# Where the stores of the first expert table are issued, and when the gathered block's pairs and rows are worked on, in a hybrid decoder step

## The chip, the core and the metric

The kernel runs on one core of a Trainium2 chip. The core has five engines with queues of their own: TensorE (PE, matrix products; its weight loads are listed as PEld), VectorE (DVE), ScalarE (ACT), GpSimd (POOL) and SyncE (SP, which only issues transfers). Each engine runs its instructions in the order of its own queue, and waits on semaphores for the others. Matrix products land in PSUM, a small memory of eight banks; all other tiles lie in SBUF; tables and intermediate results of some size lie in DRAM and are moved by DMA. A DMA is issued by an engine's queue (SP, ACT or POOL) and carried by 16 DMA engines.

The metric is the time of one execution on the device in microseconds (us); of several runs the median.

## What is computed

One inference step of a one-layer decoder for 512 prompt rows and 8 sample rows of 1024 columns. The change lies in the PEER part, a layer of 16384 small experts of which every row uses 128 (8 heads, 16 experts each):

```python
q = (xb @ peer_wq).reshape(PEER_BLOCK, PEER_HEADS, 2, PEER_QDIM // 2)
s1 = jnp.einsum('thd,hnd->thn', q[:, :, 0], peer_k1)
s2 = jnp.einsum('thd,hnd->thn', q[:, :, 1], peer_k2)
v1, i1 = lax.top_k(s1, PEER_TOPK)
v2, i2 = lax.top_k(s2, PEER_TOPK)
cand = (v1[..., :, None] + v2[..., None, :]).reshape(PEER_BLOCK, PEER_HEADS, -1)
cidx = (i1[..., :, None] * N_KEYS + i2[..., None, :]).reshape(PEER_BLOCK, PEER_HEADS, -1)
top, pos = lax.top_k(cand, PEER_TOPK)
idx = jnp.take_along_axis(cidx, pos, axis=-1)
gate = jax.nn.softmax(top.astype(jnp.float32), axis=-1).astype(xb.dtype)
act = jax.nn.gelu(jnp.einsum('thkd,td->thk', peer_u[idx], xb), approximate=False)
return jnp.einsum('thk,thkd->td', gate * act, peer_v[idx])
```

Before it in the layer come two recurrent branches (Mamba-2 and RWKV-7) and their projections, after it a small gated projection and a norm.

## The kernel before, in words

The rows are five row blocks: 0 to 3 are the 512 prompt rows, 128 each, and 4 the 8 sample rows. PEER is computed in two ways. Row blocks 0, 1, 2 and 4 (392 rows, `ND`) go the dense way: every expert's activation is computed for every row, and a gate that is zero for experts not chosen is multiplied in. Row block 3 goes the gathered way: its 128 chosen experts per row are fetched from DRAM row by row.

*The first table's loop* (L1531) runs over the 128 table blocks `i1` of `peer_u`, 128 experts each. `u_in(i1 + 1)` (L1488) loads the next block's tile `ur` (512 KB, two buffers), PE transposes it in two halves of four products into PSUM (tiles `tr` and `psB`), ACT casts each half to the high part `uh`, and DVE subtracts to get the low part `ul`. "Split" below is this pair of DVE instructions. `u_out` (L1503) makes 24 products per block (three for each of eight column groups) into `psA`; ACT applies the GELU into `ge` (three buffers), and SP stores `ge` to `ge_d` in DRAM (L1516). From block 80 (`NU`) on, the gates exist: then DVE multiplies them in ahead of the store, and the last 16 blocks stay in SBUF.

*The gates.* `pairs(pool, c, gate)` (L1321) finds, for a row block, the 16 best of 50 candidate pairs per head and their expert numbers (`ij`) and softmax weights; it is a generator in seven pieces, almost all DVE work: top-16 searches (`best16`, L1272), small index arithmetic, and two times three operations over 128x2048 elements (L1362 to L1365). `scatter` (L1376) runs `pairs` of a dense row block and then places the gates into a dense array: for four rows at a time DVE makes one-hot tiles (L1412, L1416), PE multiplies them (L1395), ACT copies the result into a staging tile `stg` (L1397), and after every 32 rows SP stores `stg`, 2 MB, to `G_d` in DRAM (L1402; 13 stores in all, the last of 0.5 MB). The pieces of the four scatters are spread over table blocks 0 to 75 by the counter `nsc` up to `NSC` (L1527, L1542): 133 pieces in 76 blocks.

*The gathered row block.* Its `pairs` run in one go ahead of the loop (`run`, L1432, called at L1440); from them come the expert numbers `e3`. `gathered` (L1447) fetches a row of 128 experts (tile `gr`, 512 KB, an indirect DMA of POOL, L1453), and DVE multiplies and sums it with the row block (L1462), for 128 rows of `peer_u` and then 128 of `peer_v`. `gather_to` (L1475) says how far it is: 80 rows over blocks 0 to 79, 70 more over blocks 80 to 127, the rest in the second table's loop (L1573), which works through `peer_v` in the same way.

*What sets the order.* A framework schedules each engine's instructions by their place in the program and their dependences, so a call's place sets the order only roughly. Each engine then keeps that order: an SP load stands behind every store that SP has ahead of it, and a store of `ge` can't go before its GELU.

The lines quoted here are the parts that the steps below use; line numbers are those of the profile.

Of the kernel before, what the change touches and what calls it, by code (L numbers as in the profile page):

```python
# [8 lines left out]
F32 = mybir.dt.float32  # L9
# [5 lines left out]
OP = mybir.AluOpType  # L15
# [15 lines left out]
def tile_hybrid(ctx: ExitStack, tc, x_prompt, x_sample, p_prompt, p_sample, state_ssm, state_conv,  # L31
# [13 lines left out]
    def f(ap):  # L45
        return ap.bitcast(F32)
# [1234 lines left out]
    with tc.tile_pool(name="qp", bufs=2, reuse_waits="tile") as qp:  # L1281
        for h in range(8):
# [9 lines left out]
            for s_ in range(2):  # L1292
                c0 = (h * 2 + s_) * P
                raw = dw.tile([P, D], F32, name="ur")
# [81 lines left out]
    def scatter(pool, c):  # L1376
# [13 lines left out]
        def place(t, one, stg):  # L1390
# [9 lines left out]
            if q + 4 == m:  # L1400
                a = off[c] + t - q
                nc.sync.dma_start(G_d[:, :, a:a + m, :].rearrange("c p t l -> p c (t l)"),  # L1402
                                  stg[:, :, :m, :].rearrange("p c t l -> p c (t l)"))
# [28 lines left out]
    def run(gen):  # L1432

        while True:
            try:
                next(gen)
            except StopIteration as e:
                return e.value

    ij = run(pairs(sc, 3, g3))  # L1440
    V.scalar_tensor_tensor(ij[:, 0], ij[:, 0], float(P), ij[:, 1], op0=OP.mult, op1=OP.add)
    S.copy(e3, ij[:, 0])
# [32 lines left out]
    def gather_to(n):  # L1475
        while rows_done[0] < n:
            next(gg, None)
            rows_done[0] += 1


    uT, vT = peer_u[0], peer_v[0]
    NU = 80
    GU1, GU2 = 80, 70
    NK = 16
    ge_d = dram.tile([P - NK, P, ND], F32, name="ge_d")
    ges = {}

    def u_in(i1):  # L1488

        raw = dw.tile([P, D], F32, name="ur")  # L1490
        nc.sync.dma_start(raw, uT[i1 * P:(i1 + 1) * P])
        uh = du.tile([P, KD, P], F32R, name="uh")
        ul = du.tile([P, KD, P], F32R, name="ul")
        for q in range(2):
            qs_ = slice(q * 4, q * 4 + 4)
            ps = pa.tile([P, 4, P], F32, name="psB") if q else pt.tile([P, 4, P], F32, name="tr")
            for k in range(4):
                T.transpose(ps[:, k], raw[:, (q * 4 + k) * P:(q * 4 + k + 1) * P], identf)
            S.copy(uh[:, qs_], ps)  # L1499
            V.tensor_tensor(ul[:, qs_], ps, f(uh[:, qs_]), op=OP.subtract)  # L1500
        return uh, ul

    def u_out(i1, u, gt):  # L1503
# [9 lines left out]
        if keep:  # L1513
            ges[i1] = a
        else:
            nc.sync.dma_start(ge_d[i1], a)  # L1516
# [6 lines left out]
    def scatters():  # L1523
        for c in (0, 1, 2, 4):
            yield from scatter(sc, c)
    sg_ = scatters()
    NSC = 4 * 6 + W0 + 3 * WAIT + 3 * 32 + 2  # L1527
    nsc = 0
    u = u_in(0)
    vbx = ExitStack()  # L1530
    for i1 in range(P):  # L1531
# [9 lines left out]
        if i1 < NU:  # L1541
# [3 lines left out]
            gather_to((i1 + 1) * GU1 // NU)  # L1545
# [171 lines left out]
```

## Time and profile before

| | us |
|---|---|
| median of 3 runs | 2987.49 |
| lowest, highest | 2976.54, 2988.84 |
| profiled execution, its own time | 2980.14 |
| its span, first to last instruction | 2978.4 |
| first table's loop, blocks 0 to 127 | about 1500 to 2322 |
| of that, blocks 0 to 79 | about 1500 to 2081 |
| second table's loop | 2322 to 2882 |

The profile is of one execution. Its views: a page with the busy share of each engine; a table of stretches, in us from the span's start; lists of who waited for whom; a timeline of each engine; and groups of instructions by line. "x24" is a count of instructions. A wait "<-DVE ul L1500" names what ended it. Durations of neighbours on an engine may overlap, since an instruction begins before the last one has drained.

### The profile page before, as it was taken

What the parts mean: (1) busy time and instruction counts of PE and PEld (TensorE: products, weight loads), DVE (VectorE), ACT (ScalarE), POOL (GpSimd) and SP (SyncE); (2) the same over time, 40 slices, a digit from 0 to 9 for tenths busy, and PEclk for the clock granted to TensorE, in tenths of its full rate; (3) what the DMA queues carried; (4) which work ended last, traced back from release to release, by engine and by line L of the source; (5) the groups of instructions that cost most, each with busy time, mean ns of one, the idle gap of its engine ahead of it and who ended that gap; (6) DMA issues with size and microseconds to landing.
All of it is one profiled execution on the core that took longest, in us unless ns stands there. A gap on an engine that the chain in (4) does not pass through costs nothing. (4 is left out here: it accounts for less than half of the span.)

```text
span 2978.4 us, 52286 instructions
## 1 busy us (share of the span) xinstructions
PE 2785.6 (94%) x20189; PEld 2594.3 (87%) x20192; DVE 2243.9 (75%) x5555; ACT 1001.0 (34%) x2027; POOL 350.2 (12%) x310
## 2 busy tenths in 40 slices
PE   5999999898997999999969999999999999999998
PEld 4988888787886888977959999999999999999986
DVE  5868787877877775345999999884777787787746
ACT  2443333334332333232223433332322333333332
POOL 0000000000000012100001111111222334322100
PEclk9999989898897999999979999999999999999999
DMA  3314252433415366541326877677998989899830
GB/s 93 80 46 109 79 122 51 107 83 87 116 44 119 81 182 186 160 135 65 89 96 218 253 232 227 217 264 224 338 333 302 332 311 328 322 317 326 276 113 29
DMA packets 446995, 528.15 MB, mean 177 GB/s; under 512 B 95464, under 2 KB 357243, under 8 KB 446705
## 3 DMA queue, kind: packets, MB, share of 16 engines
q1 hardware_dynamic: 386153, 377.42, 41.1%
q0 software_dynamic: 38304, 139.22, 13.8%
q10 hardware_dynamic: 22288, 8.16, 1.1%
q8 instruction: 159, 2.61, 0.4%
q14 instruction: 91, 0.75, 0.1%
HBM read 447.83 MB, written 77.14 MB: 176 GB/s over the span
## 5 line engine op out<-in xcount | busy, mean ns | idle before, releaser
L95 PE MATMUL ps<-hhi,whi 128*128 128x260 f32 (+1 forms) x1456 | 440.6, 303 | 7.5 <-ACT ctail L410 2.8
L97 PE MATMUL ps<-hhi,wlo 128*128 128x260 f32 (+1 forms) x1456 | 441.1, 303 | 0.8 <-DVE wlo L79 0.8
L96 PE MATMUL ps<-hlo,whi 128*128 128x260 f32 (+1 forms) x1456 | 441.2, 303 | 0.0
L97 PE MATMUL psA<-h2h,ul 128*128 128x392 f32 x1024 | 351.8, 344 | 21.6 <-DVE ul L1500 21.6
L95 PE MATMUL psA<-h2h,uh 128*128 128x392 f32 x1024 | 363.7, 355 | 0.4 <-ACT uh L1499 0.2
L97 PE MATMUL av<-ah,vl 128*128 128x392 f32 x1024 | 351.7, 344 | 1.8 <-DVE vl L79 1.8
L96 PE MATMUL psA<-h2l,uh 128*128 128x392 f32 x1024 | 352.9, 345 | 0.0
L95 PE MATMUL av<-ah,vh 128*128 128x392 f32 x1024 | 349.4, 341 | 3.2 <-ACT vh L78 3.2
L96 PE MATMUL av<-al,vh 128*128 128x392 f32 x1024 | 350.0, 342 | 1.8 <-DVE al L79 1.8
L95 PEld LDWEIGHTS ps<-hhi,whi 128*128 128x128 f32 (+1 forms) x1456 | 284.3, 195 | 20.6 <-issue 6.0
L97 PEld LDWEIGHTS ps<-hhi,wlo 128*128 128x128 f32 (+1 forms) x1456 | 283.7, 195 | 11.8 <-issue 4.5
L96 PEld LDWEIGHTS ps<-hlo,whi 128*128 128x128 f32 (+1 forms) x1456 | 284.1, 195 | 11.3 <-issue 5.5
L78 ACT CAST vh<-vr 128x1024 fp32r<-128x1024 f32 x128 | 134.1, 1050 | 316.1 <-PE av L96 150.8
L1453 POOL DMA_INDIRECT gr<-in_peer_v_dram,e x128 | 177.5, 1387 | 375.3 <-DVE o L1468 357.7
L1453 POOL DMA_INDIRECT gr<-in_peer_u_dram,e x128 | 125.9, 984 | 794.2 <-DVE junk L1462 501.4
L97 PEld LDWEIGHTS psA<-h2h,ul 128*128 128x128 f32 x1024 | 195.5, 191 | 22.1 <-DVE ul L1500 22.1
L78 ACT CAST whi<-wraw 128x1024 fp32r<-128x1024 f32 (+1 forms) x115 | 120.0, 1043 | 279.0 <-PE ps L96 231.4
L95 PEld LDWEIGHTS psA<-h2h,uh 128*128 128x128 f32 x1024 | 195.2, 191 | 1.6 <-ACT uh L1499 1.6
L95 PEld LDWEIGHTS av<-ah,vh 128*128 128x128 f32 x1024 | 193.0, 189 | 3.9 <-ACT vh L78 3.5
L79 DVE TENSOR_TENSOR vl<-vr,vh 128x1024 fp32r<-128x1024 f32 x128 | 156.2, 1222 | 52.7 <-ACT vh L78 52.6
L96 PEld LDWEIGHTS psA<-h2l,uh 128*128 128x128 f32 x1024 | 195.6, 191 | 0.0
L97 PEld LDWEIGHTS av<-ah,vl 128*128 128x128 f32 x1024 | 193.1, 189 | 2.3 <-DVE vl L79 2.3
(635 smaller groups left out, 6178.2 us busy)
## 6 DMA issues: line engine op xcount, KB each, us to landing
ur<-in_peer_u_dram SPq DMA_DIRECT2D x128, 512.0 KB
vr<-in_peer_v_dram SPq DMA_DIRECT2D x128, 512.0 KB
wraw<-in_w_in_dram SPq DMA_DIRECT2D x90, 512.0 KB
Gt<-G_d SPq DMA_DIRECT2D x32, 784.0 KB
G_d<-stg SPq DMA_DIRECT2D x12, 2048.0 KB
ge_d<-ge SPq DMA_DIRECT2D x112, 196.0 KB
gl<-ge_d SPq DMA_DIRECT2D x112, 196.0 KB
wraw<-in_w_out_ssm_dram SPq DMA_DIRECT2D x16, 512.0 KB
```

The source lines that it names most:

```text
L78: S.copy(hi, raw)
L79: eng.tensor_tensor(lo, raw, f(hi), op=OP.subtract)
L95: T.matmul(out, lhsT=a[0], rhs=b[0], start=start, stop=False)
L96: T.matmul(out, lhsT=a[0], rhs=b[1], start=False, stop=False)
L97: T.matmul(out, lhsT=a[1], rhs=b[0], start=False, stop=stop)
L1453: pin(G.indirect_dma_start(out=t, out_offset=None, in_=(peer_u, peer_v)[s_ // P][0], in_offset=bass.IndirectOffsetOnAxis(ap=e3[:, s_ % P:s ...
```

## The change

Three things are altered. First, `pairs` of the gathered row block is no longer run ahead of the loop, but becomes the first seven pieces of `scatters`, and `NSC` grows from 133 to 140; the transposes of block 0 move ahead in the text, to where `pairs` was called. Second, the gathered rows begin at the ninth table block (`NG0 = 8`): 80 rows over blocks 8 to 79 in place of 0 to 79. Third, ACT issues the stores of `G_d` and, up to block 79, those of `ge`, which SP issued; and `ur` has three buffers in place of two.

```diff
--- before.py
+++ after.py
@@ -1291,7 +1291,7 @@
             qw = []
             for s_ in range(2):
                 c0 = (h * 2 + s_) * P
-                raw = dw.tile([P, D], F32, name="ur")
+                raw = dw.tile([P, D], F32, name="ur", bufs=3)
                 kp = lambda t: t.rearrange("p (k c) -> p k c", k=KD)
                 nc.sync.dma_start(kp(raw), peer_wq[0][:, c0:c0 + P].rearrange("(k p) c -> p k c", p=P))
                 hi, lo = dw.tile([P, D], F32R, name="sh"), dw.tile([P, D], F32R, name="sl")
@@ -1399,7 +1399,7 @@
             m = min(TS, n - t + q)
             if q + 4 == m:
                 a = off[c] + t - q
-                nc.sync.dma_start(G_d[:, :, a:a + m, :].rearrange("c p t l -> p c (t l)"),
+                nc.scalar.dma_start(G_d[:, :, a:a + m, :].rearrange("c p t l -> p c (t l)"),
                                   stg[:, :, :m, :].rearrange("p c t l -> p c (t l)"))
 
         made = []
@@ -1429,17 +1429,24 @@
     sx = ExitStack()
     sc = sx.enter_context(tc.tile_pool(name="sc", bufs=1, reuse_waits="tile"))
 
-    def run(gen):
-
-        while True:
-            try:
-                next(gen)
-            except StopIteration as e:
-                return e.value
-
-    ij = run(pairs(sc, 3, g3))
-    V.scalar_tensor_tensor(ij[:, 0], ij[:, 0], float(P), ij[:, 1], op0=OP.mult, op1=OP.add)
-    S.copy(e3, ij[:, 0])
+    uT, vT = peer_u[0], peer_v[0]
+
+    def u_in(i1):
+
+        raw = dw.tile([P, D], F32, name="ur", bufs=3)
+        nc.sync.dma_start(raw, uT[i1 * P:(i1 + 1) * P])
+        uh = du.tile([P, KD, P], F32R, name="uh")
+        ul = du.tile([P, KD, P], F32R, name="ul")
+        for q in range(2):
+            qs_ = slice(q * 4, q * 4 + 4)
+            ps = pa.tile([P, 4, P], F32, name="psB") if q else pt.tile([P, 4, P], F32, name="tr")
+            for k in range(4):
+                T.transpose(ps[:, k], raw[:, (q * 4 + k) * P:(q * 4 + k + 1) * P], identf)
+            S.copy(uh[:, qs_], ps)
+            V.tensor_tensor(ul[:, qs_], ps, f(uh[:, qs_]), op=OP.subtract)
+        return uh, ul
+
+    u = u_in(0)
 
 
     AHEAD = 3
@@ -1478,27 +1485,12 @@
             rows_done[0] += 1
 
 
-    uT, vT = peer_u[0], peer_v[0]
     NU = 80
     GU1, GU2 = 80, 70
+    NG0 = 8
     NK = 16
     ge_d = dram.tile([P - NK, P, ND], F32, name="ge_d")
     ges = {}
-
-    def u_in(i1):
-
-        raw = dw.tile([P, D], F32, name="ur")
-        nc.sync.dma_start(raw, uT[i1 * P:(i1 + 1) * P])
-        uh = du.tile([P, KD, P], F32R, name="uh")
-        ul = du.tile([P, KD, P], F32R, name="ul")
-        for q in range(2):
-            qs_ = slice(q * 4, q * 4 + 4)
-            ps = pa.tile([P, 4, P], F32, name="psB") if q else pt.tile([P, 4, P], F32, name="tr")
-            for k in range(4):
-                T.transpose(ps[:, k], raw[:, (q * 4 + k) * P:(q * 4 + k + 1) * P], identf)
-            S.copy(uh[:, qs_], ps)
-            V.tensor_tensor(ul[:, qs_], ps, f(uh[:, qs_]), op=OP.subtract)
-        return uh, ul
 
     def u_out(i1, u, gt):
         uh, ul = u
@@ -1513,7 +1505,7 @@
         if keep:
             ges[i1] = a
         else:
-            nc.sync.dma_start(ge_d[i1], a)
+            (nc.scalar if gt is None else nc.sync).dma_start(ge_d[i1], a)
 
     def gates_of(ic):
         gt = vb.tile([P, ND, 4], F32, name="Gt")
@@ -1521,12 +1513,15 @@
         return gt
 
     def scatters():
+        ij = yield from pairs(sc, 3, g3)
+        V.scalar_tensor_tensor(ij[:, 0], ij[:, 0], float(P), ij[:, 1], op0=OP.mult, op1=OP.add)
+        S.copy(e3, ij[:, 0])
+        yield
         for c in (0, 1, 2, 4):
             yield from scatter(sc, c)
     sg_ = scatters()
-    NSC = 4 * 6 + W0 + 3 * WAIT + 3 * 32 + 2
+    NSC = 7 + 4 * 6 + W0 + 3 * WAIT + 3 * 32 + 2
     nsc = 0
-    u = u_in(0)
     vbx = ExitStack()
     for i1 in range(P):
         if i1 == NU:
@@ -1542,7 +1537,7 @@
             while nsc < min(NSC, NSC * (i1 + 1) // (NU - 4)):
                 next(sg_)
                 nsc += 1
-            gather_to((i1 + 1) * GU1 // NU)
+            gather_to(max(0, i1 + 1 - NG0) * GU1 // (NU - NG0))
         else:
             gather_to(GU1 + (i1 + 1 - NU) * GU2 // (P - NU))
     px.close()
```

On SP, where the scattering is under way before: `G_d` is the gates' store, `ge_d` the activations', `ur` the table's loads, `x2` two in a row.

```order
L1402 DMA G_d<-stg 128x32x128
L1516 DMA ge_d<-ge 128x392
L1491 DMA ur<-in_peer_u_dram 128x1024 x2
L1516 DMA ge_d<-ge 128x392
L1491 DMA ur<-in_peer_u_dram 128x1024
```

And SP now, from the end of the stage before (`kr` and the first `ur` are loads of that stage) to the first gates that are read back (`Gt`):

```order
L1296 DMA ur<-in_peer_wq_dram 128x8x128
L1437 DMA ur<-in_peer_u_dram 128x1024
L1288 DMA kr<-in_peer_k_dram 128x128 x2
L1437 DMA ur<-in_peer_u_dram 128x1024 x84
L1512 DMA Gt<-G_d 128x1568 x2
L1508 DMA ge_d<-ge 128x392
```

The stores no longer stand between the loads; 84 loads follow one another.

On ACT, at the same place of the loop before (`gs` is the PSUM tile of the placed gates, L1510 the GELU, L1499 the casts of a block two ahead):

```order
L1510 ACTIVATE ge<-psA 128x392
L1397 COPY stg<-gs 128x4x32x4 x2
L1499 CAST uh<-tr 128x512
L1499 CAST uh<-psB 128x512
L1510 ACTIVATE ge<-psA 128x392
```

and around the first store of `G_d` now (L1502 is the GELU, L1445 the casts):

```order
L1502 ACTIVATE ge<-psA 128x392
L1508 DMA ge_d<-ge 128x392
L1397 COPY stg<-gs 128x4x32x4
L1402 DMA G_d<-stg 128x32x128
L1397 COPY stg<-gs 128x4x32x4
L1445 CAST uh<-tr 128x512
L1445 CAST uh<-psB 128x512
L1502 ACTIVATE ge<-psA 128x392
```

The two stores now stand in ACT's queue, ahead of the copies and casts.

On DVE, the rows ahead of the split of block 3 before (the end of `pairs` of the gathered row block, L1441 its last row, with the searches of row block 0 among it):

```order
L1365 TENSOR_REDUCE ij<-eq 128x128
L1326 CAST fi<-i_0_15736 128x256
L1441 SCALAR_TENSOR_TENSOR ij<-ij 128x128
L1279 MAX_INDEX pos<-top,rest 128x8
L1274 MAX top<-cand 128x8 x2
```

and, in the order now, the middle of the same `pairs`, with half of the split of block 5 in it:

```order
L1362 TENSOR_TENSOR eq<-iota,ab 128x2048
L1352 TENSOR_TENSOR ab<-ab,ge__17547 128x128
L1364 TENSOR_TENSOR eq<-eq,fi 128x2048
L1354 TENSOR_SCALAR ge__17547<-pf 128x128
L1365 TENSOR_REDUCE ij<-eq 128x128
L1355 TENSOR_SCALAR ge__17547<-ge__17547 128x128
L1446 TENSOR_TENSOR ul<-psB,uh 128x512
```

The splits of blocks 3, 4 and 5, which stood behind the whole of these `pairs`, now stand among its rows.

## Rows read from the trace of the kernel before

**Rows 1.** Page, part 1: busy us (share of the span) and instructions of each engine.

```profile
PE 2785.6 (94%) x20189; PEld 2594.3 (87%) x20192; DVE 2243.9 (75%) x5555; ACT 1001.0 (34%) x2027; POOL 350.2 (12%) x310
```

**Rows 2.** Stretches of the first table's loop: busy us of each engine (instructions).

```profile
core 0: us, PE busy (x) PEld busy (x) DVE busy (x) ACT busy (x) POOL busy (x), PEclk, DMA share, GB/s
1511.00:1798.00 287.00, 255.11 (x1648) 251.74 (x1649) 279.56 (x909) 100.29 (x182) 40.63 (x41) 0.94 0.67 213
1798.00:1965.00 167.00, 157.50 (x1039) 156.68 (x1038) 146.98 (x362) 58.98 (x110) 24.87 (x24) 0.97 0.73 230
1965.00:2081.00 116.00, 107.99 (x701) 106.76 (x700) 65.82 (x143) 36.06 (x70) 16.93 (x17) 0.97 0.76 243
2081.00:2322.00 241.00, 241.00 (x1493) 239.23 (x1492) 174.94 (x259) 70.24 (x140) 64.51 (x68) 1.00 0.92 323
```

**Rows 3.** Waits of PE, 1480 to 2330: us in total, times, longest us.

```profile
PE tr L1498 <- DMA ur<-in_peer_u_dram: 25.2, 9, 6.4
PE psA L97 <- DVE ul L1500: 21.6, 2, 21.2
```

**Rows 4.** Timeline of PE: start, us, instruction [idle before <- what ended it].

```profile
1551.70 0.70 PE L97 MATMUL psA<-h2h,ul 128*128 128x392 f32 x1 [21.16 <-DVE ul L1500]
...
1720.75 1.08 PE L1498 MATMUL tr<-identf,ur 128*128 128x128 f32 x4 [4.51 <-DMA ur<-in_peer_u_dram]
...
2036.35 1.09 PE L1498 MATMUL tr<-identf,ur 128*128 128x128 f32 x4 [6.36 <-DMA ur<-in_peer_u_dram]
```

**Rows 5.** Short stretches, same columns as rows 2.

```profile
1512.00:1553.00 41.00, 19.84 (x104) 19.14 (x104) 40.67 (x201) 10.92 (x16) 1.99 (x2) 0.71 0.26 81
...
1718.00:1726.00 8.00, 5.25 (x21) 5.28 (x22) 4.91 (x27) 1.17 (x2) 0.56 (x1) 0.57 0.63 232
...
2032.00:2040.00 8.00, 3.65 (x16) 3.68 (x17) 1.38 (x2) 1.17 (x2) 0.00 (x0) 0.57 0.67 215
```

**Rows 6.** Groups by line on DVE, 1511 to 1553: count | busy us, mean ns.

```profile
L1364 DVE TENSOR_TENSOR eq<-eq,fi 128x2048 f32<-128x2048 f32 x2 | 4.6, 2284 | 0.0
L1365 DVE TENSOR_REDUCE ij<-eq 128x128 f32<-128x2048 f32 x2 | 4.6, 2278 | 0.0
L1362 DVE TENSOR_TENSOR eq<-iota,ab 128x2048 f32<-128x2048 f32 x2 | 4.6, 2277 | 0.0
```

**Rows 7.** Timeline of SP at two stores, and all stores of one kind (min/median/max ns).

```profile
1705.86 0.38 SPq L1402 DMA_DIRECT2D G_d<-stg  x1
1710.93 2.35 SPq L1516 DMA_DIRECT2D ge_d<-ge  x1
1713.37 1.27 SPq L1491 DMA_DIRECT2D ur<-in_peer_u_dram  x2
...
1861.90 0.38 SPq L1402 DMA_DIRECT2D G_d<-stg  x1
1866.96 6.02 SPq L1516 DMA_DIRECT2D ge_d<-ge  x1
...
L1516 SPq DMA_DIRECT2D ge_d<-ge x112: 319/326/6415, 1520.1 to 2242.2; - x112
```

**Rows 8.** Groups by line on DVE, 1500 to 2087: count | busy us, mean ns | idle before.

```profile
L1416 DVE TENSOR_SCALAR o<-iota,tT 128x128 f32<-128x128 f32 x392 | 111.5, 340 | 14.3 <-PE gs L1395 14.0
L1462 DVE SCALAR_TENSOR_TENSOR junk<-gr,xn 128x1024 bf16<-128x1024 f32 x77 | 93.7, 1217 | 0.1
L1412 DVE TENSOR_TENSOR o<-iota,tT 128x512 f32<-128x512 f32 x98 | 66.8, 682 | 3.7 <-ACT tT L1388 3.6
```

**Rows 9.** Timelines of DVE, PE and ACT around one block of the scattering.

```profile
1661.43 0.68 DVE L1500 TENSOR_TENSOR ul<-psB,uh 128x512 fp32r<-128x512 f32 x1
...
1665.99 0.43 PE L95 MATMUL psA<-h2h,uh 128*128 128x392 f32 x1
...
1663.61 0.50 ACT L1510 ACTIVATE ge<-psA 128x392 f32<-128x392 f32 x1 [3.59 <-PE psA L97]
```

**Rows 10.** Landings of the gathered tile `gr`, issue to landing.

```profile
DMA to landing us min/median/max: 4.1/6.4/12.4
```

**Rows 11.** A store that ACT's queue issues in an earlier stage (min/median/max ns).

```profile
L1069 ACTq DMA_DIRECT2D g_d<-dtmp x16: 321/327/350, 1005.9 to 1151.7; - x16
```

## The prediction

> **What bounds the kernel now.** I read the page's busy shares first: TensorE (PE) 94% of the span, VectorE (DVE) 75% [rows 1]. A share over the whole span doesn't say what a change in one stage is worth, so the second view is the table of stretches over the first table's loop [rows 2]. In the last of them, blocks 84 to 127, PE is busy for 241 of 241 us and issues 1492 weight loads; a block has 32 (24 of products, 8 of transposes), so a block costs 241 / 1492 x 32 = 5.17 us of PE and nothing else bounds that stretch. The scattering stretch before it is different: from 1511 to 1798 DVE is busy for 279.6 of 287 us while PE misses 32, from 1798 to 1965 DVE has 147.0 of 167, and from 1965 to 2081 DVE has only 65.8 of 116 and is no limit. So up to 1965 (there DVE makes the low half of block 64) two engines are nearly full, and after it PE alone counts.
>
> The third view is the list of waits on PE [rows 3]: over the whole loop PE waits on two things, 25.2 us for the transposed table tile `ur` to land (nine times) and 21.6 us for `ul`, the low half that DVE makes of a block. The timeline shows where [rows 4]: 21.16 us in one piece ending at 1551.7, and of the `ur` waits the first long one, ending at 1720.7, and the longest and last, ending at 2036.4; two more long ones end at 1844.6 and 1878.3.
>
> The 21 us are the gathered block's `pairs`. DVE works through 1512 to 1553 almost without a break, 40.7 of 41 us [rows 5]; each index half takes three 128x2048 operations of 2.28 us [rows 6], 13.7 us for the two halves, and most of the rest is the top-k. The split of block 3 stands behind all of it. The `ur` waits are the SP queue [rows 7]: at 1705.9 SP issues a 2 MB store of `G_d`; behind it stands a store of `ge` that can't go before the GELU and takes 2.35 us to issue; the two loads of `ur` go out at 1713.4, 7.5 us after the store, and their data stand behind its 2 MB on the same queue. PE waits to 1720.7. At 1861.9 the same, with a store that takes 6.02 us.
>
> **The change, part by part.** *The pairs move into the loop.* Before, all of `pairs` precedes the split of block 3 in DVE's order; now the seven pieces go to blocks 0 to 3, and splits stand between them. DVE's work isn't less, so PE can't win the whole 21 us at once: blocks 1 to 9 now carry both `pairs` of the gathered block and of block 0. What is less, for a time, is gathering. Counted in the order of instructions up to the split of block 16, DVE has 8 gather rows fewer ahead of it (4 for 12), 24 of the 128x128 one-hots and 6 of the 128x512 ones. By start-to-start steps of about 1.15, 0.26 and 0.60 us (durations 1.217, 0.340 and 0.682, and neighbours overlap by 0.07 to 0.08 [rows 8]) that is 9.2 + 6.2 + 3.6 = 19 us. So block 16 can come up to 19 us earlier, against the 21.6 that PE waited there; I take 15, because PE will still wait for splits in blocks 5, 6 and 9, where the order, summed the same way, leaves 11 to 12 us of DVE work between two splits (PE's block is 5.2).
>
> *The stores move to ACT; the loads are three deep.* SP then issues nothing but 84 loads of `ur` in a row, each as soon as a buffer is free, three blocks ahead: 3 x 5.17 = 15.5 us at least. No row shows an SP load beside a store on ACT's queue. The nearest row for its landing is the gather, also 512 KB, on a queue of its own while SP's queue holds those same stores: 4.1 to 12.4 us [rows 10]. Below 15.5, so I count all nine waits as gone: 25.2 us. The clock adds to it: behind each of the four longest waits the granted clock falls, to 0.57 on average in the stretch around the resumption after the first and the last of them, a mixture of 1.2 and 2.4 GHz [rows 5]; there 22 and 17 weight loads took 5.28 and 3.68 us, where the 0.16 us of the full stretch (5.17 / 32) make 3.6 and 2.7: 1.7 and 1 us more, so some 5 for the four. Together 30 us, of which 8 (the last, 6.4, and two small ones) and 1 of clock lie behind 1965.
>
> *DVE caps the sum.* At block 64 the same DVE work stands ahead of the split in either order (59 gather rows for 60, 84 one-hot groups for 83, all ten index halves). It was busy for 279.6 + 147.0 = 426.6 us of the 454 up to there [rows 2]; block 64 can come at most 27.4 us earlier, though PE's own waits before it come to 21.6 + 17.2 + 4 of clock = 43. DVE will not run without a gap either: in its fullest stretch it kept 7.4 us of idle time. So up to 1965 I take 27.4 - 7.4 = 20 us (bounds: 7.4, if the 20 idle us after 1798 stay, and 27.4). Behind 1965 PE alone counts and the 9 us are won in full. 20 + 9 = 29 us.
>
> *What ACT pays.* It issues 92 DMAs more. A store of ACT's own of before takes 0.327 us in its queue [rows 11], so 92 x 0.33 = 30 us on an engine that is 35% busy there (100.3 of 287 us [rows 2]). That is covered by ACT's wait for the block's last product, 3.59 us in the block shown [rows 9]. Not covered is a store of `ge` that doesn't get out because a `G_d` is ahead of it: on SP it took 0.319 to 6.415 us [rows 7]. Behind it on ACT now stand the copies out of PSUM and the casts `uh` of the next block but one; for these DVE's split waits, and for that PE. The slack is in the timeline: the split of a block ends at 1662.11 and PE starts that block at 1665.99 [rows 9]: 3.9 us. Only the stalls above it cost: two of the thirteen, of 6.0 and 6.4, lose some 2 us each, and the others took 0.3 to 3.6; I take 3 in all, rounded down for what DVE's own lateness hides. If the cover were gone, all 13 stores at 6.4 would cost 13 x (6.4 - 3.9) = 33.
>
> *Nothing else.* The gather still stands at row 80 after block 79, its first row needs `e3` by block 8, and the order makes that between the splits of blocks 5 and 6. From block 80 on, the order is the same, so what the loop wins arrives at the end: 29 - 3 = 26 us.
>
> **The rivals.** (a) *The loads still come late.* The store's 2 MB and a load of `ur` need the same 16 DMA engines, so another queue may help nothing. Then the 30 us stay and only the pairs' part is won: 15 us, less 3 for ACT: 2968. For it: the DMA share is 0.67 to 0.76 in the stretch [rows 2]. Against it: the gathers' 12.4 us, and that before a load left 7.5 us late. The Trainium skill has this rule, page "DMA: Bandwidth & Descriptors", section "Issuing engines are not separate DMA queues": DMAs from several engines run on the same 16 engines and interleave, and issuing from several saves only the sequencer's time. The same page, section "Queues, rings and completion order", says that a DMA engine alternates between its queues packet by packet, by which a load would not stand behind 2 MB of another queue. By the one rule the time is (a)'s 2968, by the other the forecast's; the gathers agree with the second, and no run here has yet shown SP beside ACT.
>
> (b) *DVE takes over.* PE's waits for `ur` gave DVE time to catch up; without them PE waits for `ul` instead, and the idle 20 us of DVE after 1798 stay. Then 7.4 + 9 - 3 = 13 us: 2967. For it: DVE is 97% busy up to 1798. Against it: those 20 us fell largely beside PE's waits for `ur`, when `uh` came late.
>
> (c) *Slower: ACT holds back PE.* If ACT's store of `ge` gets out only when the `G_d` ahead of it has nearly landed, which now shares the engines with the `ur` loads, every one of 13 stalls ACT. The store is issued some 5 us after `G_d`; with X us to its release PE loses X - 5 - 3.9 each time. The 29 us are gone at X = 11.1; at 14 the loss is 13 x 5.1 = 66 and the time 2980 - 29 + 66 = 3017. On SP the slowest two were released at 11.1 and 11.5, the one at 1710.9 at 7.4, the others by about 8 [rows 7].
>
> (d) *All of it.* DVE runs on without a gap and ACT costs nothing: 27.4 + 9 = 36 us: 2944.
>
> **How the numbers follow.** The profiled execution took 2980.1 us (span 2978.4 and 1.7 around it). The median of the three runs is 2987.5, the lowest 2976.5, so the profiled one stands near the fast end, and a median can come out some 7 us above my sum. Forecast: 2980 - 26 = 2954, chance 0.60 (own range 2940 to 2964). (a) 0.11, (b) 0.12, (c) 0.06, (d) 0.11. A measurement of this kernel tells about 0.5% (15 us) from no change. Forecast and (d) are faster by more, 0.71, and of (a) and (b) with 12 to 15 us somewhat over a third, 0.09; the rest of them is within 0.5%, as 0.14; (c) is slower, 0.06. For the range I go from 2932, below (d) by what the runs differ, to 2974, above (a) and (b) with part of the runs' spread; (c) and a run at the slow end lie outside.
>
> **What the profile after would show.** Pairs: no wait of 21 us for `ul`, but several of 3 to 7 between blocks 4 and 10. Stores: PE's waits for `ur` under 3 us in all, SP's loads 0.33 us each; a clock of 1.00 from 1600 on. Cap: DVE over 95% busy up to block 64, the loop's last block some 26 us earlier. ACT: stores of `ge` of 0.33 us, a few of 3 to 6. I am wrong if the `ur` waits remain (a), if the waits for `ul` add up to over 20 us (b), or if ACT's stores take over 6 us after every `G_d` (c).

## The result, and the profile of the changed kernel

The changed kernel takes 2951.39 us (median of 4 runs, 2946.46 to 2953.89) beside 2984.73 for the kernel before on the same chip (4 runs, 2976.54 to 2988.84): a ratio of 0.9887, 95% interval 0.9871 to 0.9902. The forecast was 2954. The profiled execution took 2951.08 us, its span 2949.4, where that of before was 2978.4.

The page's busy line, to be laid beside [rows 1] (engine, busy us, share of the span, instructions):

```profile
PE 2779.3 (94%) x20189; PEld 2584.2 (88%) x20192; DVE 2239.9 (76%) x5555; ACT 1000.7 (34%) x2027; POOL 362.3 (12%) x310
```

Nothing is gone from any engine: the instructions are the same in number, and 29 us of the span are waits and half-speed clock that are no longer there. The list of waits on PE from 1480 to 2310 us answers [rows 3] (us in total, times, longest):

```profile
PE psA L97 <- DVE ul L1446: 19.7, 10, 7.7
...
PE psA L95 <- ACT uh L1445: 2.2, 3, 1.2
```

No line for `ur` is left in it; before, it was the longest. The 21-us wait for `ul` has become ten shorter ones, of which the timeline of PE shows the two that come first, 1.32 and 7.70 us, where [rows 4] had 21.16:

```profile
1547.56 0.45 PE L97 MATMUL psA<-h2h,ul 128*128 128x392 f32 x1 [1.32 <-DVE ul L1446]
...
1558.83 0.70 PE L97 MATMUL psA<-h2h,ul 128*128 128x392 f32 x1 [7.70 <-DVE ul L1446]
```

Stretches of the loop, same columns as [rows 2], whose four the first four lines answer. The fifth lies around the gathered block's pairs, as the first of [rows 5]; the sixth is there for its clock; the seventh reaches from DVE's split of block 0 to that of block 64:

```profile
1514.00:1801.00 287.00, 274.00 (x1784) 271.23 (x1785) 284.95 (x914) 107.20 (x195) 39.56 (x39) 0.97 0.69 221
1801.00:1943.00 142.00, 135.66 (x905) 133.37 (x904) 136.15 (x346) 51.49 (x96) 26.08 (x24) 1.00 0.75 245
1943.00:2058.00 115.00, 113.40 (x746) 111.92 (x745) 71.26 (x156) 39.00 (x76) 21.06 (x20) 1.00 0.84 271
2058.00:2294.00 236.00, 233.88 (x1447) 231.75 (x1445) 173.62 (x257) 67.43 (x134) 64.50 (x68) 1.00 0.91 320
1514.00:1556.00 42.00, 34.66 (x196) 33.52 (x196) 41.16 (x185) 14.30 (x26) 0.00 (x0) 0.91 0.41 130
...
1600.00:1801.00 201.00, 198.57 (x1349) 197.67 (x1348) 200.09 (x583) 79.04 (x145) 33.72 (x33) 1.00 0.80 254
...
1516.02:1947.24 431.22, 412.57 (x2713) 407.51 (x2712) 423.32 (x1264) 159.52 (x292) 67.40 (x64) 0.98 0.72 230
```

Up to 1801 DVE is busy for 284.95 of 287 us, and PE for 274 where it was 255. The granted clock is 1.00 (2.4 GHz) from 1600 us on; in three of the four stretches of before it was 0.94 or 0.97. DVE made the split of block 64 431.2 us after that of block 0; the same stretch of the kernel before is this row:

```profile
1513.08:1964.70 451.62, 410.98 (x2680) 406.78 (x2679) 424.16 (x1263) 158.96 (x291) 65.50 (x65) 0.95 0.69 219
```

DVE kept its work, 423 for 424 us, and gave up 20 us of idle time.

What ACT and SP issue now: the stores of `ge` and the loads of `ur`, 1514 to 2110 us (min/median/max ns of an issue), beside [rows 7]:

```profile
L1508 ACTq DMA_DIRECT2D ge_d<-ge x80: 326/326/9637, 1522.3 to 2043.8; - x80
...
L1437 SPq DMA_DIRECT2D ur<-in_peer_u_dram x92: 327/328/412, 1515.8 to 2105.1; - x92
```

SP's loads go out without a stall, and the stalls that [rows 7] showed on SP are on ACT. Its timeline shows the longest, and below it DVE's and PE's rows that follow from it:

```profile
1850.84 0.38 ACTq L1402 DMA_DIRECT2D G_d<-stg  x1
...
1855.96 9.64 ACTq L1508 DMA_DIRECT2D ge_d<-ge  x1
1865.64 0.59 ACT L1445 CAST uh<-psB 128x512 fp32r<-128x512 f32 x1 [9.23 <-issue]
...
1866.26 0.69 DVE L1446 TENSOR_TENSOR ul<-psB,uh 128x512 fp32r<-128x512 f32 x1 [4.39 <-ACT uh L1445]
...
1866.28 0.45 PE L95 MATMUL psA<-h2h,uh 128*128 128x392 f32 x1 [0.79 <-ACT uh L1445]
```

ACT stands for 9.23 us behind its own store, its next cast `uh` is late, DVE waits 4.39 us for that cast and PE 0.79. Of the twelve stores of `ge` that follow a `G_d` on ACT, three took 0.3 to 1.1 us, six 2.1 to 4.1, and three 5.61, 8.13 and 9.64.

**A second measure.** The loop's first GELU starts at 1518.8 us in the trace of before and at 1521.8 in that of after; over all the traces below it lies between 1511.3 and 1526.4, though the stages ahead of it differ in little but `ur`'s buffers. So beside the medians I compare the time from the GELU of block 0 to the GELU of block 127, the "loop". It is that of one profiled execution of each kernel, and no kernel was profiled twice. What follows the loop is the same program in all thirteen traces and took 655.1 to 660.0 us, so I call no difference of under 5 us shown by the loop alone. Before it is 803.6 us; after, by the first and the last of these rows of ACT's timeline, 772.5, or 31.1 us less:

```profile
1521.77 0.50 ACT L1502 ACTIVATE ge<-psA 128x392 f32<-128x392 f32 x1 [4.05 <-PE psA L97]
...
2294.28 0.50 ACT L1502 ACTIVATE gek<-psA 128x392 f32<-128x392 f32 x1 [3.79 <-PE psA L97]
```

### The profile page after: what moved, and what is told of

It is laid out like the page before. It is cut to its first block, busy times and chain, and to the rows that moved or that the text cites. A ratio compares the mean times of both kernels' runs of the same rounds, so it can differ in the third digit from the quotient of the medians.

```text
span 2949.4 us, 52302 instructions
## 1 busy us (share of the span) xinstructions
PE 2779.3 (94%) x20189; PEld 2584.2 (88%) x20192; DVE 2239.9 (76%) x5555; ACT 1000.7 (34%) x2027; POOL 362.3 (12%) x310
## 5 line engine op out<-in xcount | busy, mean ns | idle before, releaser
L97 PE MATMUL psA<-h2h,ul 128*128 128x392 f32 x1024 | 351.8, 344 | 19.9 <-DVE ul L1446 19.7
L1460 POOL DMA_INDIRECT gr<-in_peer_v_dram,e x128 | 186.0, 1453 | 368.9 <-DVE o L1475 353.4
L96 PEld LDWEIGHTS av<-al,vh 128*128 128x128 f32 x1024 | 192.5, 188 | 1.7 <-DVE al L79 1.7
## 6 DMA issues: line engine op xcount, KB each, us to landing
Gt<-G_d SPq DMA_DIRECT2D x32, 784.0 KB
```

The lines of the kernel that those rows point to most:

```text
L96: T.matmul(out, lhsT=a[0], rhs=b[1], start=False, stop=False)
L97: T.matmul(out, lhsT=a[1], rhs=b[0], start=False, stop=stop)
L1460: pin(G.indirect_dma_start(out=t, out_offset=None, in_=(peer_u, peer_v)[s_ // P][0], in_offset=bass.IndirectOffsetOnAxis(ap=e3[:, s_ % P:s ...
```

## The experiments

All of them at a glance. "Won" is by the medians against the kernel before on the same chip (2982.1 to 2984.7 us), then by the loop of one profiled execution; the two agree within 6 us everywhere.

| kernel | ratio, 95% interval | median, us | won, us | loop, us | won, us |
|---|---|---|---|---|---|
| changed kernel | 0.9887 (0.9871 to 0.9902) | 2951.4 | 33 | 772.5 | 31.1 |
| before, `ur` three deep | 0.9894 (0.9875 to 0.9913) | 2951.4 | 33 | 776.4 | 27.2 |
| before, `G_d` on ACT | 0.9922 (0.9903 to 0.9942) | 2959.5 | 24 | 779.5 | 24.1 |
| before, `G_d` and `ge` on ACT, `ur` three deep | 0.9921 (0.9907 to 0.9934) | 2962.3 | 22 | 784.0 | 19.6 |
| before, pairs spread | 0.9948 (0.9934 to 0.9961) | 2967.9 | 16 | 785.9 | 17.7 |
| changed, `ur` two deep | 0.9910 (0.9896 to 0.9925) | 2954.6 | 27 | 776.5 | 27.1 |
| changed, all stores on SP | 0.9880 (0.9863 to 0.9896) | 2948.1 | 34 | 769.0 | 34.6 |
| changed, `G_d` on SP | 0.9863 (0.9848 to 0.9878) | 2944.2 | 40 | 768.0 | 35.6 |
| changed, `ge` on SP | 0.9866 (0.9850 to 0.9883) | 2940.5 | 42 | 765.4 | 38.2 |
| changed, `G_d` on SP, slow start | 0.9845 (0.9830 to 0.9861) | 2936.5 | 46 | 759.3 | 44.3 |
| changed, `ge` on SP, slow start | 0.9844 (0.9822 to 0.9866) | 2936.9 | 47 | 757.0 | 46.6 |
| the same, 64 rows gathered by block 79 | 0.9830 (0.9810 to 0.9851) | 2932.2 | 51 | 757.0 | 46.6 |

### What removes the waits for `ur`

**The third buffer alone**, against the kernel before, at both places where `ur` is made:

```diff
-        raw = dw.tile([P, D], F32, name="ur")
+        raw = dw.tile([P, D], F32, name="ur", bufs=3)
```

> The kernel before with ur three deep and nothing else. Theory (the loads stand behind the stores in SP's order, and this order is the same): a third buffer doesn't let a load go out ahead of the store of ge that it is queued behind; the four long ur waits stay, the small ones may go: gain 0 to 6 us, 2979 to 2985, ratio 0.998 to 1.000. Rival (the third buffer is what removes the waits, a load being 5.2 us earlier than before): waits for ur fall from 25 to under 8 us, gain 20, 2965, ratio 0.993.

Measured: 2951.4 us, ratio 0.9894. The rival holds, with more won than it said, and my theory fell: one word wins as much by the medians as the whole change. The waits on PE from 1514 to 2290 us (the second line is a wait of the same kind, its end put down to "issue"):

```profile
PE tr L1498 <- DMA ur<-in_peer_u_dram: 3.1, 2, 1.7
PE tr L1498 <- issue: 2.0, 1, 2.0
```

SP's timeline at the fourth `G_d` of this run shows why I had misread the order:

```profile
1701.23 0.38 SPq L1402 DMA_DIRECT2D G_d<-stg  x1
1706.29 2.37 SPq L1516 DMA_DIRECT2D ge_d<-ge  x1
1708.76 1.31 SPq L1491 DMA_DIRECT2D ur<-in_peer_u_dram  x2
```

It is the picture of [rows 7], within a few hundredths of a microsecond: the store takes 2.37 us (2.35 before), the two loads go out 7.5 us after `G_d`. But they are other loads. Counted along the trace, 29 loads of `ur` and 26 stores of `ge` stand ahead of this `G_d` before, and 30 and 26 now; ahead of each of the thirteen it is one load more. An order that reads the same row for row can be shifted by one. What is held behind `G_d` is now needed one block later: from issue to the GELU of its block a load has 30.3 us (median of blocks 20 to 74), and had 24.2.

**The queue alone**, the kernel before with

```diff
-                nc.sync.dma_start(G_d[:, :, a:a + m, :].rearrange("c p t l -> p c (t l)"),
+                nc.scalar.dma_start(G_d[:, :, a:a + m, :].rearrange("c p t l -> p c (t l)"),
```

> The kernel before with the 13 stores of G_d on ACT's queue and nothing else: ur two deep, ge on SP, pairs in one piece. Theory (queue and third buffer are two cures for one thing, a load of ur that is held by 2 MB ahead of it on its queue; either is enough, and ACT pays only where a store of its own stands behind G_d): waits for ur fall from 25 to under 5 us, no loss on ACT; from the first block to the last the loop is 25 to 30 us shorter, as with the third buffer alone (27): 2955 to 2960, ratio 0.990 to 0.992. Rival (the stores of ge hold the loads as much as G_d does): waits for ur of 10 us or more, ratio 0.993 to 0.998.

Measured: 2959.5, ratio 0.9922, the loop 24.1 us shorter. PE's waits, 1514 to 2290 us:

```profile
PE psA L97 <- DVE ul L1500: 27.7, 7, 21.1
...
PE tr L1498 <- DMA ur<-in_peer_u_dram: 1.3, 2, 1.0
```

Two buffers are enough once the 2 MB are on another queue; the theory holds (the loop just short of its 25 to 30 us), and the stores of `ge`, still on SP, do not bring the waits back. Part of the gain has turned into waits for `ul`, 27.7 us where it was 21.6.

**Everything but the third buffer**: the changed kernel with `ur` as before.

```diff
-        raw = dw.tile([P, D], F32, name="ur", bufs=3)
+        raw = dw.tile([P, D], F32, name="ur")
```

> The changed kernel with ur two deep, as before; all stores of G_d and ge up to block 79 stay on ACT. The theory of the prediction (the waits for ur come from SP's queue, where the loads stand behind stores): with a queue of their own two buffers are nearly enough, waits for ur under 5 us, 2950 to 2955, ratio 0.987 to 0.990. Rival (the lead of a load decides, whatever queue the stores are on): waits for ur of 10 to 25 us, and ACT's stalls besides, 2962 to 2975, ratio 0.992 to 0.997.

Measured: 2954.6, ratio 0.9910, waits for `ur` of 4.0 us in five pieces. The first theory holds. So queue and third buffer are two cures for one thing, and either takes away 20 to 24 of the 25 us. On top of the other the third buffer is worth 4 us of the loop (27.1 to 31.1), within its scatter; on top of the third buffer, as the next group shows, the move of the stores brings nothing more.

### What the stores cost on ACT

**The stores and the buffer, without the pairs**: the kernel before with the third buffer, `G_d` on ACT as above, and

```diff
-            nc.sync.dma_start(ge_d[i1], a)
+            (nc.scalar if gt is None else nc.sync).dma_start(ge_d[i1], a)
```

> The kernel before with the stores of G_d and of ge (blocks 0 to 79) on ACT's queue and ur three deep; the pairs stay in one piece ahead of the loop and the gathering begins at block 0. Theory (the parts aren't additive, DVE caps both at block 64): the 21-us wait for ul stays, all ur waits (25 us, and 5 of clock) go; DVE has the same work ahead of the split of block 64, so up to 1965 us the gain is the cap's 20 us, behind it 9, less 3 for ACT: 26 us, 2959 us, ratio 0.991. Rival A (parts add up): the changed kernel won 33, of which the pairs 15, so this one wins 18: 2967, ratio 0.994. Rival B (the loads were late for another reason than SP's queue): no gain, 2985 to 2990, ur waits of 25 us still there.

Measured: 2962.3, ratio 0.9921, the loop 19.6 us shorter. The time lies between the theory's and rival A's and doesn't tell them apart, but the trace does. From the split of block 0 to that of block 64:

```profile
1520.58:1967.05 446.47, 415.25 (x2726) 410.68 (x2725) 426.96 (x1275) 160.60 (x295) 71.02 (x66) 0.96 0.70 227
```

That is 5.2 us less than before, not 20, and DVE was idle for 19.5 of it: it waited 11.7 us for the placed gates of PE (`gs`) and 5.6 for `uh`. So in this run DVE's work was not the cap, and the theory's mechanism fell. The run tells something else besides: with the third buffer alone the loop was 27.2 us shorter, so the stores on ACT take 7.6 us away (11 by the medians, with intervals that just overlap).

**`ge` back on SP**, `G_d` left on ACT: the diff above, undone, in the changed kernel.

> The changed kernel with the stores of ge back on SP; G_d stays on ACT. Then nothing that ACT issues stands behind a G_d, and SP has stores but no 2 MB. Theory (the changed kernel pays for stores of ge that ACT can't get out behind G_d, 40 us above 0.33 each in all, of which PE sees 4 to 7): no wait for uh and fewer for ul, 2943 to 2948, ratio 0.986 to 0.988, as with G_d on SP. Rival (what G_d costs on ACT is not a stall of the queue, but something that any queue beside SP's would bring, its data beside the loads): 2951, ratio 0.989, as the changed kernel.

Measured: 2940.5, ratio 0.9866; the loop is 7.1 us shorter than the changed kernel's (the intervals of the medians overlap). The theory holds: what costs is not that `G_d` is on ACT but that a store of `ge` stands behind it there. How it costs is in DVE's waits, from 1514 to 1950 us, of the changed kernel and then of this one:

```profile
DVE ul L1446 <- ACT uh L1445: 5.0, 2, 4.4
```

```profile
DVE ul L1446 <- ACT uh L1445: 0.7, 2, 0.5
```

and in this run's stretch from the split of block 0 to that of block 64:

```profile
1505.71:1931.39 425.68, 410.71 (x2712) 407.30 (x2711) 422.45 (x1263) 160.76 (x294) 66.80 (x64) 0.98 0.73 233
```

425.7 us, with 3.2 of DVE idle, where the changed kernel had 431.2 with 7.9: of the 5.5 us between them 4.7 are idle time of DVE, and 4.3 of that is waiting for `uh`. Behind block 64, where DVE has time, the stalls of ACT cost next to nothing (342.7 and 343.0 us from there to block 127), though one of 8.13 us is among them.

**`G_d` back on SP**, `ge` left on ACT: the diff of `G_d`, undone, in the changed kernel.

> The changed kernel with only the store of G_d back on SP: ge stays on ACT, ur stays three deep, pairs spread. The loads have 2 MB ahead of them on their queue at each of the 13 places, but no store that must wait for the GELU; ACT has no store behind G_d. Theory: ACT's stalls are gone (4 us won against the changed kernel), a load 15.5 us ahead outlasts the 11 us that the slowest release took, so waits for ur stay under 5 us: 2945 to 2955, ratio 0.987 to 0.990. Rival A (data behind 2 MB on the same queue is late whatever is issued): waits for ur of 10 to 25 us come back, 2960 to 2975, ratio 0.992 to 0.997. Rival B (ACT's stalls cost over 10 us in the changed kernel): 2940, ratio 0.985.

Measured: 2944.2, ratio 0.9863, between the theory's 2945 and rival B's 2940. The loop is 4.5 us shorter than the changed kernel's, where the theory said 4 and rival B over 10; the stores of `ge` on ACT now take 0.327 us at most, and PE waits 5.5 us for `ur`, hardly more than the 5 of the theory and half of the least that rival A named. What stands behind `G_d` is now a load, and it is held in its turn (all loads of `ur`, 1514 to 2110 us; and one `G_d` with the three loads behind it):

```profile
L1437 SPq DMA_DIRECT2D ur<-in_peer_u_dram x94: 327/328/12442, 1514.9 to 2108.4; - x94
```

```profile
1845.19 0.38 SPq L1402 DMA_DIRECT2D G_d<-stg  x1
1845.66 13.81 SPq L1437 DMA_DIRECT2D ur<-in_peer_u_dram  x3
```

The first of the three took 12.44 us to go out, and PE waited 4.3 us for it, the longest wait for `ur` in this run. Twelve more places of this kind, with holds of 0.7 to 10.8 us, cost PE 1.2 us in all: a load that is three deep has the time.

**All stores back on SP**, third buffer and spread pairs left.

> The changed kernel with all its stores back on SP: left of the change are ur three deep, the spread pairs and the gathering from the 9th block on. The theory as the first four runs leave it (the third buffer is what removes the ur waits, ACT's part of the change only costs, DVE caps the rest): the third buffer alone left DVE 8.4 us of idle time up to block 64, and by the new order DVE has 6 us less to do up to there, so the pairs can add up to 14 us; beside the run with only ge on ACT, 2944 us, ratio 0.985 to 0.988. Rival (a store of ge behind G_d on SP holds the loads of ur again, and it was the move of ge that freed them): ur waits of over 10 us, 2952 to 2960, ratio 0.989 to 0.992.

Measured: 2948.1, ratio 0.9880 (0.9863 to 0.9896). The time lies at the upper end of the theory's range, its interval takes in the lower end of the rival's; the waits for `ur` and the loop, 34.6 us shorter, speak for the theory:

```profile
PE tr L1444 <- DMA ur<-in_peer_u_dram: 6.2, 2, 5.3
```

Beside the changed kernel (31.1) the two moves of stores to ACT are no gain; a loss of 3.5 us is too small to be called shown.

### What the spread pairs bring

**The pairs alone**: the changed kernel with the stores on SP and `ur` two deep.

> The changed kernel with its stores back on SP and ur two deep: of the change only the spread pairs and the gathering from the 9th block on are left. Theory: 15 us by block 16 and no more behind it, ur waits of some 25 us as before: 2970 us, ratio 0.995. Rival A (additive): the same 15 us, 0.995; it differs from the theory in the other part's run, and in the sum of the two parts: 41 us by the theory, 33 by this. Rival B (DVE only shifts its work): what PE wins at block 4 it waits for ul again by block 64, gain 0 to 5: 2980 to 2985, ratio 0.998 to 1.000.

Measured: 2967.9, ratio 0.9948. By block 16 the loop is 21.0 us shorter (124.9 to 103.9 from the GELU of block 0), at block 64 21.7, at the end 17.7; the waits for `ur` are still there:

```profile
PE tr L1444 <- DMA ur<-in_peer_u_dram: 22.1, 7, 7.3
```

Theory and rival A gave the same number and rival B fell. The sum with the stores and the buffer, 17.7 and 19.6, is 37.3, where both together won 31.1: less than the sum, but ACT's stalls and the scatter of the loop could make up the 6 us. The third buffer and the pairs, both with the stores on SP, decide it. Alone they bring 27.2 and 17.7 us of the loop, together 34.6; by the medians 33 and 16, together 34. At the split of block 64 each alone came 20 us earlier (431.5 and 431.6 us for 451.6); added up that would be 411.5. The run with both has this row there:

```profile
1514.74:1937.56 422.82, 407.24 (x2675) 404.73 (x2674) 416.49 (x1251) 157.90 (x290) 61.73 (x63) 0.97 0.73 232
```

DVE alone has 416.5 us to do, more than the 411.5: so the parts can't add up, and DVE's work is the reason. Laid on the third buffer the pairs bring 7.4 us, not 17.7.

### Where the cap is

**A slow start**: the changed kernel with `G_d` on SP, and one piece of the scattering a block for eight blocks.

```diff
-            while nsc < min(NSC, NSC * (i1 + 1) // (NU - 4)):
+            while nsc < (i1 + 1 if i1 < 8 else min(NSC, 8 + (NSC - 8) * (i1 - 7) // (NU - 12))):
```

> The changed kernel with G_d on SP (2944 us) and, in the first eight blocks, one piece of the scattering's work a block in place of 1.76; the rest catches up later (1.85 a block). Theory (DVE has more to do than PE only in blocks 3 to 9; 9.4 us of PE's waits for ul are there): these 9.4 us go, but DVE was idle for only 3.3 us up to block 64, so a part comes back as waits for ul further on: gain 3 to 9, 2935 to 2941, ratio 0.983 to 0.986. Rival (DVE's sum up to block 64 decides alone): all of it comes back, 2944, ratio 0.986 to 0.988.

Measured: 2936.5, ratio 0.9845; the loop is 8.7 us shorter than without the slow start, and PE's waits for `ul` fall from 12.2 to 4.1 us. Nothing of it came back:

```profile
PE psA L97 <- DVE ul L1446: 4.1, 4, 2.1
```

But the run doesn't part the two explanations as I had meant it to: the edit also leaves 10 us less DVE work ahead of the split of block 64 (407.4 for 417.9), and the GELU of block 64 comes 10.2 us earlier. Both explanations fit that.

**The two best edits together**: `G_d` on ACT, `ge` on SP, slow start.

> The changed kernel with ge on SP (G_d on ACT) and the slow start of one piece a block in the first eight blocks. Theory: the two gains stand on different things (ACT's stalls; DVE's pile in blocks 3 to 9) and add: the loop is 38 us shorter than before with the one, the other was worth 9: 47 us, 2933 to 2938, ratio 0.982 to 0.985. Rival (DVE's sum up to block 64 is the limit in both): no more than the slow start had with G_d on SP, 44 us, and waits for ul of over 10 us come back between blocks 10 and 64.

Measured: 2936.9, ratio 0.9844, the loop 757.0: 46.6 us less than before, beside the theory's 47 and the rival's 44. Neither the loop nor the medians tell it from the run ahead; PE's waits for `ul`, against the rival's over 10 us, speak for the theory:

```profile
PE psA L97 <- DVE ul L1446: 5.0, 8, 1.3
```

**And less gathering ahead of block 80**, in that kernel:

```diff
-    GU1, GU2 = 80, 70
+    GU1, GU2 = 64, 86
```

> The run with G_d on ACT, ge on SP and the slow start, and besides 64 gathered rows up to block 79 and 86 behind it, where it had 80 and 70: some 13 rows of 1.15 us less, 15 us, on DVE ahead of the split of block 64. Theory (with the slow start PE waits for little more than 5 us in the loop, and PE is then what bounds it): gain 0 to 5 us, 2930 to 2935, ratio 0.981 to 0.984, DVE's idle time up to block 64 rises from 3 to some 15 us. Rival (DVE's sum still caps the loop): gain 10 to 15 us, 2921 to 2926, ratio 0.978 to 0.980. Against both: rows that are now gathered beside the last 48 blocks delay PE there, and the gain is below nothing.

Measured: 2932.2, ratio 0.9830, and the same loop, 757.0 us. From the split of block 0 to that of block 64, first without the edit, then with it:

```profile
1510.66:1921.19 410.53, 402.35 (x2659) 397.68 (x2658) 407.62 (x1236) 157.22 (x288) 69.22 (x63) 0.99 0.74 238
```

```profile
1507.16:1919.11 411.95, 402.47 (x2656) 398.56 (x2655) 403.17 (x1217) 157.28 (x288) 53.16 (x50) 0.99 0.70 222
```

DVE has 4.5 us less to do, not the 15 I had expected (13 gathered rows are gone from ahead of the split, but one index half of a row block's `pairs` has come there), and its idle time rises from 2.9 to 8.8 us; the stretch doesn't get shorter. PE is busy for 402 of 411 us in both: at 98% it bounds this stretch, as the theory said, and the rest are short waits for DVE. The 5 us between the medians are inside the intervals. With ratios of 0.983 to 0.9845 the last three kernels are faster than both the kernel before and the changed one, whose intervals they don't touch.

## Why the prediction came out, step by step

**The total** was right: 26 us forecast against the profiled execution, 29 in the span, 31 in the loop, 33 by the medians. That the time itself came within 3 us (2951.4 for 2954) is in part luck: I subtracted from an execution of 2980, 4.6 us below the median of before (2984.7). And two of the terms were off in opposite directions.

**The pairs.** "So block 16 can come up to 19 us earlier ... I take 15". It came 21 us earlier in the run with the pairs alone. The time between DVE's splits of blocks 0 and 16 fell from 121.0 to 100.2 us, nearly all of it busy (118.0 and 98.6): 19 us of work less, as the count of operations had said. The 4 us that I took off for PE's waits in blocks 5, 6 and 9 were a mistake: PE did wait near there (9.8 us in one piece), but in a stretch where DVE works without a gap PE's waits are a result of DVE's sum and not a loss beside it.

**The stores and the buffers.** "I count all nine waits as gone: 25.2 us" is what happened, 0 of 25.2 left. The row that I took the landing from, the gather on a queue of its own, pointed the right way. But the step priced two edits as one. The runs show that either does it, the buffer leaving 5 us and the queue 1, and that the third buffer needed no other queue. And of the two reasons that the prediction gave for a late load, only one shows. I timed the DMA packets of `ur` in the traces, at the twelve 2 MB stores of the kernel before and of the one with `G_d` alone moved. Before, the next load had left SP 8.6 us after `G_d` was issued (mean; 7.4 to 12.0) and landed 4.7 us later (3.4 to 6.1). With `G_d` on ACT it had left after 0.8 us (0.6 to 1.5) and landed 5.4 us later (3.7 to 8.4). So the late issue is what was saved; "their data stand behind its 2 MB" is so in the packets, but a load on a queue without them landed no faster. These are packets, MB and share of one queue: SP's (q1) from 1714.7 to 1717 us before, when the two loads of [rows 7] had left and only 512-byte packets of the store went, then ACT's (q10) and SP's from 1703 to 1707 with `G_d` on ACT, the store and one whole load beside each other:

```profile
q1 hardware_dynamic: 278, 0.14, 20.8%
...
q10 hardware_dynamic: 1538, 0.79, 71.1%
q1 hardware_dynamic: 144, 0.52, 33.2%
```

**The cap.** "So up to 1965 I take 27.4 - 7.4 = 20 us": measured at the split of block 64, 451.6 - 431.2 = 20.4, with 7.9 us of DVE idle left. The number came out by luck. The 7.4 us that I let DVE keep were mostly waits for `uh`, as this line of the kernel before shows (1511 to 1798 us):

```profile
DVE ul L1500 <- ACT uh L1499: 6.0, 5, 2.9
```

In the changed kernel 5.0 of the 7.9 us are waits for `uh` again, but now behind ACT's own stores, a loss that I had priced apart. With `ge` on SP 3.2 us of idle time are left, and the split comes 25.9 us earlier, near the upper bound of 27.4. So this term was too small by about 6, ACT's by 4, and the two errors cancel in part.

This was the term that kept the sum from the 36 us of case (d), and it is why parts that win 27 and 18 alone win 35 together on SP. The same rows say how to move it: it is a cap on the work ahead of block 64. The order of the slow start left 407.6 us of it there, and block 64's split came at 410.5.

**Behind 1965** I took 9 us. From the GELU of block 64 to that of 127 it is 5.1 (348.1 to 343.0), and up to that GELU 26.0. The difference to 20.4 is the boundary: DVE was 9.6 us ahead of the GELU at block 64 before and 4.0 after, and that lead is what PE had spent. Both together are 31.1 with ACT's loss already in them, where I had 29 without it and 26 with it; without the loss (`ge` on SP) the loop won 38.2.

**ACT** is the other term that was mis-sized: 3 forecast, 7.1 measured (the changed kernel against `ge` on SP), 7.6 without the pairs. The rule of the step was nearly right: what the stalls of 4.07, 5.61, 8.13 and 9.64 have above 3.9 us comes to 11.9 us, and to 7.6 without that of 8.13, which lies behind block 64. Wrong were two choices. I carried SP's stalls of before over to ACT, where the longest is 9.64 and not 6.4; not all of that is ACT's, for in the new order with all stores on SP the longest is 8.07. And I "rounded down for what DVE's own lateness hides", which is the wrong way round: where DVE is the cap, what it waits for `uh` counts, whether PE has slack or not: 4.3 of the 5.5 us by which the split of block 64 came later are such waits.

**The rivals.** (a) fell: with `G_d` on another queue and nothing else, 24 us were won. The sentence of the Trainium skill that speaks for it (page "DMA: Bandwidth & Descriptors", section "Issuing engines are not separate DMA queues": issuing from several engines saves only the sequencer's time) holds in kind: by the packets above the issue is what was saved. But the page calls this time usually small beside the DMA itself, and here it was 8.6 us (SP's wait for the GELU ahead of the store of `ge` is in it) beside 4.7 from there to the landing. The other rule, of queues that alternate, shows in the last two lines of packets; it is not what the time was won by. (b) did not come about, narrowly: the waits for `ul` add up to 19.7 us, where I had put the sign at 20; but DVE's idle time did go. (c) had the mechanism and not the size: measured from the issue of `G_d`, the twelve stores were released after 6.6 to 14.8 us, 9.0 in the mean, below the break-even of 11.1, and behind block 64 they cost next to nothing.

**The signs** named for the profile after: waits for `ur` under 3 us, loads of 0.33 us, a clock of 1.00 from 1600 on and DVE over 95% busy up to block 64 (99%, then 96%) are all there; the loop's end came 28 us earlier, for 26. The "several of 3 to 7 between blocks 4 and 10" were one of 7.7, one of 1.3 and one of 0.4, and the "few of 3 to 6" reached 9.64.

## What to carry to other kernels

Before a store is moved to another engine's queue, ask what will stand behind it there: a load with blocks to spare costs little, an engine that computes pays for its own next DMA. When two edits aim at one wait, try the smaller alone; here one more buffer was worth nearly the whole change, and an order that looks unchanged row for row had moved every load up by one place. And where an engine is the cap, count what its feeders make it wait, not what its reader has in hand.

## What the runs showed of the hardware

The next DMA that an engine issues behind the 2 MB store is held, whatever it is and whichever engine issues it: a store of `ge` on SP up to 8.07 us (with all stores back there), on ACT up to 9.64, a load of `ur` on SP up to 12.44. Counted from the issue of `G_d` the hold ended after 5.8 to 12.9 us on SP (with the loads right behind it) and after 6.6 to 14.8 on ACT, longest at the same places of the program in both (the 8th, 10th and 12th `G_d`). It goes with the store's own progress: in the packets of these two traces 2,450 to 3,390 of the store's 4,096 had started by then, at the long holds as at the short ones. Why the store is slower at those places is not shown. And a held DMA holds its engine: ACT ran nothing for 9.23 us.

The loop doesn't start at the same time: its first GELU lies between 1511.3 and 1526.4 us over these traces, 15 us, as much as half of what the change won. Why is not shown.
